# A hybrid SSD and attention layer: products with the states made channel-major, decays as rows from DRAM, the skip inside the decay matrix

## The chip, the cores and the metric

The kernel runs on one core of one Trainium2 chip. The metric is the device time of one execution in microseconds (us), lower is better. Three runs of the kernel before took 1216.43, 1216.73 and 1217.33 us, so the median is 1216.73 us. In the profile PE is the matrix engine TensorE, PEld its loading of weights, DVE is VectorE, ACT is ScalarE, POOL is GpSimd and SP is SyncE, which here issues most of the DMAs.

## The reference

One layer over 512 latent tokens with 1024 channels, and 256 context tokens that are only read. A combined projection feeds two mixers, an SSD (state space) branch that runs in both directions and a windowed attention, which are gated, merged, projected and followed by a gated ConvFFN. The change concerns only the output of the SSD branch. It has 32 heads of 64 channels in 4 groups, a state of 128 and chunks of 128 tokens:

```python
    decay_to_end = jnp.exp(cs[..., -1:] - cs)
    states = jnp.einsum('bcsgn,bgrcs,bcsgrp->bcgrpn', bc, decay_to_end, xc)
    ...
    cb = jnp.einsum('bclgn,bcsgn->bgcls', cc, bc)
    scores = cb[:, :, None] * jnp.exp(segsum(ac))
    y_diag = jnp.einsum('bgrcls,bcsgrp->bclgrp', scores, xc)
    y_off = jnp.einsum('bclgn,bcgrpn,bgrcl->bclgrp', cc, states[:, :-1], jnp.exp(cs))
    return (y_diag + y_off).reshape(Bsz, L, G, R, P).astype(xs.dtype), final
...
    y = yf + jnp.flip(yb, axis=1) if with_output else None
...
    y = y + d_skip.reshape(SSD_GROUPS, SSD_HPG, 1).astype(y.dtype) * xs
    return rmsnorm(y.reshape(Bsz, L, D_SSD) * jax.nn.silu(z), g)
```

For every chunk and group there are thus three parts: what the tokens of the chunk give each other (`y_diag`, in both directions), what the forward and the backward state give, each scaled by a decay per token and head (`y_off`), and the skip `d_skip * xs`. Their sum is multiplied by silu(z).

## The kernel before

The large products run on PE in three passes of a float32 split into a high and a low part (`gemm`, L238, L239, L241); the weights come by SP's queue into `wraw` (L177), ACT casts the high part `whi` (L183) and DVE subtracts for the low part `wlo` (L184). Before the SSD stand the modulation, the attention with most other projections beside it, and a stage that works out the decay tables: `tables` makes the cumulative sums `cs`, their exponential `U` (ACT) and more; `table_turns` turns `dt`, `U`, `X` and `la` so that tokens lie on partitions (three PE transposes each and two copies on ACT), into `TT`, `TU`, `TX` and `TD`. `cs` also goes to DRAM (`cs_d`).

The SSD itself lasts from about 430 to 720 us. The list `prog` takes the four groups one after the other and puts one projection of the next group (in the last group, a gate projection) behind each chunk: states, then for chunk c = 0 to 3 `chunk_out(c)`, `chunk_in(c+1)` and one projection step. A scheduler then orders the instructions of each engine, within what the program's dependencies allow; small pieces in the list `BETWEEN` are set by hand into the middle of a projection.

- `chunk_in(c)` prepares the decay matrices. Two DMAs broadcast rows of `cs_d` into `fb`. `products` makes B·C for the chunk on PE (`cb`, L1664), takes its diagonal on DVE (`cbd`, L1666) and makes `coef` on POOL (L1670, L1671): the diagonal of the backward direction plus the skip, one number for each token and head. `decays` adds on ACT (L1680, L1683), joins both directions on DVE (L1684) and takes the exponential on ACT (L1687) into two tiles `E` of four heads each. `weighed` multiplies `E` by `cb` on DVE (L1691). In three of four chunks (0 + 1 + 1 + 2 times a group) it also issues `square`: ACT squares a finished tile of the group before (L1558) into one buffer, and POOL adds it to `ssq` (L1559).
- `chunk_out(c)` makes two products with the states on PE, tokens on partitions (L1707: C is the stationary operand, the state with 512 columns moves through), which DVE scales by `TU` into two tiles `te` (L1709). Sixteen passes (L1715) make `yd`, channels on partitions, from `xs` and `E`. POOL makes `dx = xs*coef` (L1717) and adds both `te` (L1718, L1720). Then the state moves on (POOL L1581, PE L1579, DVE L1582). `late` adds `dx` to `yd` by four PE transposes (L1728) that accumulate in PSUM, and DVE multiplies by z (L1730).

A plain float32 product of PE shows as two passes in the trace, each with its own load of weights; a transpose is one pass.

## Time and profile before

| | |
|---|---|
| median of three runs | 1216.73 us |
| span of the profiled execution (first to last instruction) | 1215.7 us |
| TensorE clock granted in it | 1.000 |
| bytes moved by DMA | 215.74 MB, 177 GB/s on the mean |
| SSD part, 440 to 720 us: POOL busy | 116.4 of 280 us |
| SSD part: DVE busy | 221.2 of 280 us |

The profile gives no time of the profiled execution beside its span. The median of the runs lies 1.0 us above that span, and 1.0 us is taken as what lies around it. Busy time is counted from an instruction's start to its end, and the ends of the matrix engine's passes are modelled. What a pass costs is therefore read from the distance between two starts.

### The profile page before, as it was taken

The numbers are of one execution on the slowest core, as the hardware profiler recorded it, in microseconds if no ns is written. First come the engines' busy times: TensorE is split into PE (matmuls) and PEld (weight loads), VectorE is DVE, ScalarE is ACT, GpSimd is POOL, SyncE is SP. The second block draws the span as 40 slices with busy tenths as digits, with TensorE's granted clock in tenths as the row PEclk, the third lists the DMA queues.
The fourth block names the chain that finished last, engine by engine and source line by source line (L and its number), as shares of the span: only waits on it lengthen the run. The fifth ranks groups of instructions, "written<-read, shape, count | busy, mean of one in ns | idle before, by whom it ended". The sixth has DMA issues, their size and how long they took to land.

```text
span 1215.7 us, 17471 instructions
## 1 busy us (share of the span) xinstructions
PE 1208.4 (99%) x6288; PEld 992.9 (82%) x6288; DVE 923.6 (76%) x1494; ACT 683.4 (56%) x1269; POOL 220.9 (18%) x242
## 2 busy tenths in 40 slices
PE   9999999999999999999999999999999999999998
PEld 6798888888878877778787778888988888888886
DVE  5857888888565688697896867677687777778787
ACT  5557787778544367476575664223543443436654
POOL 0000121100102534252451622000200100110021
PEclk9999999999999999999999999999999999999999
DMA  9655889834758525356366558777266634436662
GB/s 371 258 139 184 160 239 263 170 139 137 170 154 257 172 85 175 116 128 202 96 160 207 171 186 273 242 232 249 51 161 149 194 118 135 133 105 222 214 185 98
DMA packets 124424, 215.74 MB, mean 177 GB/s; under 512 B 26697, under 2 KB 69745, under 8 KB 124337
## 3 DMA queue, kind: packets, MB, share of 16 engines
q1 hardware_dynamic: 110256, 187.09, 49.1%
q0 software_dynamic: 13792, 27.27, 9.9%
q8 instruction: 49, 0.80, 0.3%
q14 instruction: 39, 0.31, 0.1%
q10 hardware_dynamic: 288, 0.27, 0.1%
HBM read 187.78 MB, written 44.89 MB: 191 GB/s over the span
## 4 chain that ended last, share of the span: by engine, by line
PE 98%; issue 1%; DVE 0%; ACT 0%; POOL 0%; DVEq 0%; POOLq 0%; ACTq 0%
PE acc L238 20%; PE acc L241 20%; PE acc L239 20%; PE score L978 3%; PE po L1027 3%; PE pt L1014 2%; PE mis L581 2%; PE mis L1707 2%; PE mis L1579 2%; PE mis L2244 2%; PE mis L2245 2%; PE mis L2243 2%; PE mis L1715 1%; PE acc L2244 1%; PE acc L2245 1%; PE acc L2243 1%
## 5 line engine op out<-in xcount | busy, mean ns | idle before, releaser
L183 ACT CAST whi<-wraw 128x1024 fp32r<-128x1024 f32 (+1 forms) x115 | 120.3, 1047 | 159.3 <-PE acc L239 104.7
L184 DVE TENSOR_TENSOR wlo<-wraw,whi 128x1024 fp32r<-128x1024 f32 (+1 forms) x115 | 144.7, 1259 | 68.2 <-ACT whi L183 65.8
L238 PE MATMUL acc<-hlh,whi 128*128 128x512 f32 x472 | 193.9, 411 | 0.0
L239 PE MATMUL acc<-hll,whi 128*128 128x512 f32 x472 | 184.9, 392 | 0.0
L241 PE MATMUL acc<-hlh,wlo 128*128 128x512 f32 x472 | 184.9, 392 | 0.0
L241 PE MATMUL acc<-mh,wlo 128*128 128x512 f32 x368 | 143.3, 389 | 0.0
L238 PE MATMUL acc<-mh,whi 128*128 128x512 f32 x368 | 143.3, 389 | 0.0
L239 PE MATMUL acc<-ml,whi 128*128 128x512 f32 x368 | 143.2, 389 | 0.0
L241 PEld LDWEIGHTS acc<-hlh,wlo 128*128 128x128 f32 x472 | 88.6, 188 | 19.5
L238 PEld LDWEIGHTS acc<-hlh,whi 128*128 128x128 f32 x472 | 88.8, 188 | 17.9 <-issue 2.8
L239 PEld LDWEIGHTS acc<-hll,whi 128*128 128x128 f32 x472 | 88.9, 188 | 17.4 <-issue 2.4
L241 PEld LDWEIGHTS acc<-mh,wlo 128*128 128x128 f32 x368 | 69.1, 188 | 14.9 <-DVE wlo L184 0.5
L239 PEld LDWEIGHTS acc<-ml,whi 128*128 128x128 f32 x368 | 69.1, 188 | 14.4
L238 PEld LDWEIGHTS acc<-mh,whi 128*128 128x128 f32 x368 | 69.1, 188 | 14.2
L987 DVE CUSTOM_DVE_ANT_0 p<-score,winm,nsink 128x512 f32<-128x512 f32 (+1 forms) x64 | 51.8, 810 | 15.3 <-PE score L978 13.8
L1412 DVE SCALAR_TENSOR_TENSOR ta<-acc,half,ta 128x511 f32<-128x511 f32 (+1 forms) x66 | 43.8, 664 | 23.2 <-ACT ta L1411 23.0
L164 POOL DMA_DIRECT2D dsum<-wdn x24 | 25.4, 1146 | 193.1 <-DVE wlo L1111 171.8
L1411 ACT ACTIVATE ta<-acc,half 128x512 f32<-128x512 f32 (+1 forms) x66 | 46.8, 710 | 24.3 <-PE acc L241 23.0
L994 ACT ACTIVATE p<-p,mneg 128x512 f32<-128x512 f32 (+1 forms) x64 | 49.7, 777 | 15.4 <-DVE mneg L987 14.8
L1022 DVE TENSOR_TENSOR ptl<-pt,pth 128x512 fp32r<-128x512 f32 x72 | 47.5, 685 | 8.7 <-ACT pth L1018 7.7
L238 PE MATMUL acc<-hch,whi 128*128 128x256 f32 x176 | 53.2, 302 | 0.0
L812 DVE SCALAR_TENSOR_TENSOR tm<-wraw,csil,tm 128x512 f32<-128x512 f32 x56 | 43.1, 770 | 12.7 <-DMA wraw<-wm 12.0
(454 smaller groups left out, 3011.1 us busy)
## 6 DMA issues: line engine op xcount, KB each, us to landing
wraw<-wup SPq DMA_DIRECT2D x44, 512.0 KB, 3.8
dsum<-wdn POOLq DMA_DIRECT2D x24, 704.0 KB, 8.7
wraw<-wm SPq DMA_DIRECT2D x32, 512.0 KB, 3.6
fb<-cs_d SPq DMA_DIRECT2D x32, 512.0 KB, 6.6
wraw<-wx SPq DMA_DIRECT2D x24, 512.0 KB, 3.6
wm<-wm SPq DMA_DIRECT2D x16, 512.0 KB, 8.3
wraw<-wz SPq DMA_DIRECT2D x16, 512.0 KB, 4.3
wraw<-wos SPq DMA_DIRECT2D x16, 512.0 KB, 4.7
```

What stands on the lines that cost most here:

```text
L183: F["cast"] = S.copy(hi[:, :n], r[:, :n])
L184: F["sub"] = V.tensor_tensor(lo[:, :n], r[:, :n], raw(hi[:, :n]), ALU.subtract)
L238: T.matmul(ps, wh, xh[:, k0 + k, :], start=a, stop=False)
L239: T.matmul(ps, wh, xl[:, k0 + k, :], start=False, stop=False)
L241: T.matmul(ps, wl, xh[:, k0 + k, :], start=False, stop=b)
L812: V.scalar_tensor_tensor(acc, r[:, u * 512 : u * 512 + 512], sc, acc, ALU.mult, ALU.add)
L987: V.tensor_tensor_reduce(p[:, :w], d["ps"][i][:, o0 : o0 + w], m, op0=ALU.add, op1=ALU.min, scale=1.0, scalar=nsink[:, h : h + 1], accum_o ...
L994: S.activation(p, p, AF.Exp, bias=d["mneg"][:, i : i + 1], scale=-1.0, accum_out=d["den"][:, i : i + 1])
L1022: V.tensor_tensor(d["ptl"][x], d["pt"][x], raw(d["pth"][x]), ALU.subtract)
L1411: S.activation(o[:, :n], ps[:, :n], AF.Identity, scale=hcol(base_w, stride + i), bias=hcol(base_b, i))
L1412: x = V.scalar_tensor_tensor(o[:, 1:n], ps[:, 0 : n - 1], hcol(base_w, i), o[:, 1:n], ALU.mult, ALU.add)
L2243: T.matmul(ps, h, wh, start=st, stop=False, skip_group_check=True)
```

## The change

Three things are done for every chunk and group.

The products with the states are made with channels on partitions. Each becomes four products with 128 columns of the state as the stationary operand and C as the moving one (L1738 in the changed kernel, in place of L1707). The decay per token must now lie along the free axis: `far_out` writes `U` to DRAM (`us_d`), and four DMAs a chunk read it back as rows, each broadcast over 64 partitions, into two tiles `far` (three buffers). The table `TU`, its three transposes and its two copies go.

For chunks 1 to 3 `coef` enters the decay matrix: POOL makes two tiles `dg` (identity times `coef`) and, behind DVE's `weighed`, adds them to `E`. The four transposes of `late` then go; chunk 0 keeps `dx` and its transposes. POOL's two adds of `te` become one (`y`), DVE adds `yd` to it, and the multiplication by z moves from DVE to POOL.

The scratch of the software DMA queue (POOL's) is set to 4096 bytes a partition. Left out of the diff: the new DRAM tile, the list of table turns without `U`, and the tile `TU`.

```diff
+        def far_out():
+            for a in range(2):
+                for x in range(2):
+                    (r0, r1), n = rows(a, x), 128 if x else 384
+                    nc.sync.dma_start(us_d[32 * a : 32 * a + 32, 384 * x : 384 * x + n], d["U"][r0:r1, :n])
...
-        op("20", "ACT", 1.8, act("U", "cs", AF.Exp), ["17", "e1"])
+        op("20", "ACT", 1.8, lambda: (act("U", "cs", AF.Exp)(), far_out()), ["17", "e1"])
...
+            far = []
+            for dr in range(2):
+                f = bp.tile([P, 4, P], F32, tag="far", name="far", bufs=FAR)
+                for u in range(2):
+                    a = bass.AP(
+                        tensor=us_d.tensor,
+                        offset=us_d.offset + (32 * dr + 8 * g + u) * L + c * P,
+                        ap=[[0, 64], [2 * L, 4], [1, P]],
+                    )
+                    nc.sync.dma_start(f[64 * u : 64 * u + 64], a)
+                far.append(f)
+            d["far", c] = far
...
+                d["dg"] = [diagonal(q) for q in range(2)] if c else None
+
+            def diagonal(q):
+                dg = bp.tile([P, 4, P], F32, tag="dg", name="dg", bufs=2)
+                w = d["coef"][:, 4 * q : 4 * q + 4].unsqueeze(2).to_broadcast([P, 4, P])
+                G.tensor_tensor(dg, ident.unsqueeze(1).to_broadcast([P, 4, P]), w, ALU.mult)
+                return dg
...
-                for E in d["E"]:
+                for q, E in enumerate(d["E"]):
                     V.tensor_tensor(E, E, d["cb"][:, :P].unsqueeze(1).to_broadcast([P, 4, P]), ALU.mult)
+                    if c:
+                        G.tensor_tensor(E, E, d["dg"][q], ALU.add)
...
-                T.matmul(ps, d["CT"][:, tok], s, start=True, stop=True)
+                for ct in range(4):
+                    z = slice(ct * P, (ct + 1) * P)
+                    T.matmul(ps[:, z], s[:, z], d["CT"][:, tok], start=True, stop=True)
                 t = tmp("te")
-                V.tensor_tensor(h8(t), h8(ps), bc64(TU[:, c, dr, 8 * g : 8 * g + 8]), ALU.mult)
+                V.tensor_tensor(t, ps, flat(far[dr]), ALU.mult)
...
-            dx = bp.tile([P, 512], F32, tag="tf", name="dx", bufs=1)
-            G.tensor_tensor(h8(dx), h8(xs[:, c, :]), bc64(coef), ALU.mult)
-            G.tensor_tensor(dx, dx, parts[1], ALU.add)
-            y = dx
-            G.tensor_tensor(dx, dx, parts[0], ALU.add)
+            dx = None
+            if not c:
+                dx = bp.tile([P, 512], F32, tag="dx", name="dx", bufs=1)
+                G.tensor_tensor(h8(dx), h8(xs[:, c, :]), bc64(d["coef"]), ALU.mult)
+            y = bp.tile([P, 512], F32, tag="tf", name="y", bufs=1)
+            G.tensor_tensor(y, parts[0], parts[1], ALU.add)
...
-                for ct in range(4):
+                for ct in range(0 if c else 4):
                     z = slice(ct * P, (ct + 1) * P)
-                    tc.keep_in_program_order(T.matmul(yd[:, z], y[:, z], ident, start=False, stop=ct == 3, is_transpose=True))
+                    tc.keep_in_program_order(T.matmul(yd[:, z], dx[:, z], ident, start=False, stop=ct == 3, is_transpose=True))
+                V.tensor_tensor(y, yd, y, ALU.add)
                 z = d["zt"][:, :, tok]
-                V.tensor_tensor(z, yd.rearrange("p (a t) -> p a t", a=4), z, ALU.mult)
+                G.tensor_tensor(z, y.rearrange("p (a t) -> p a t", a=4), z, ALU.mult)
...
-    nc = bacc.Bacc("TRN2", target_bir_lowering=False, num_devices=1)
+    nc = bacc.Bacc("TRN2", target_bir_lowering=False, num_devices=1, dynamic_dma_scratch_size=4096)
```

The order of the built program shows where the new instructions stand. On PE, in the last group between chunks 2 and 3, before:

```order
L239 MATMUL acc<-hll,whi 128x512
L241 MATMUL acc<-hlh,wlo 128x512
L1728 MATMUL mis<-ident,dx 128x128 x4
L1707 MATMUL mis<-st,CT 128x512 x2
L1715 MATMUL mis<-E,xs 64x128 x8
L238 MATMUL acc<-hlh,whi 128x512
```

and in the changed kernel, at the same place:

```order
L239 MATMUL acc<-hll,whi 128x512
L241 MATMUL acc<-hlh,wlo 128x512
L1738 MATMUL mis<-CT,st 128x128 x8
L1746 MATMUL mis<-E,xs 64x128 x8
L238 MATMUL acc<-hlh,whi 128x512
```

The four transposes are gone, and two products with 512 columns have become eight with 128. The products with `E` (L1746) now follow an add on POOL.

On POOL, in the third group (group 2), from the adds of chunk 1's `te` to those of chunk 2's, before:

```order
L1718 TENSOR_TENSOR dx<-dx,te 128x512
L1720 TENSOR_TENSOR dx<-dx,te 128x512
L1559 TENSOR_TENSOR ssq<-ssq,sq 128x512
L1581 TENSOR_TENSOR st<-st,eT 128x512
L1670 TENSOR_SCALAR coef<-TT,cbd 128x8
L1671 TENSOR_TENSOR coef<-coef,bcs 128x8
L1559 TENSOR_TENSOR ssq<-ssq,sq 128x512 x2
L1717 TENSOR_TENSOR dx<-xs,coef 128x512
L1718 TENSOR_TENSOR dx<-dx,te 128x512
```

and in the changed kernel:

```order
L1752 TENSOR_TENSOR y<-te 128x512
L1567 TENSOR_TENSOR ssq<-ssq,sq 128x512
L1589 TENSOR_TENSOR st<-st,eT 128x512
L1690 TENSOR_SCALAR coef<-TT,cbd 128x8
L1691 TENSOR_TENSOR coef<-coef,bcs 128x8
L1697 TENSOR_TENSOR dg<-ident,coef 128x512 x2
L1763 TENSOR_TENSOR zs<-y,zs 128x4x128
L1567 TENSOR_TENSOR ssq<-ssq,sq 128x512
L1720 TENSOR_TENSOR E<-E,dg 128x512 x2
L1567 TENSOR_TENSOR ssq<-ssq,sq 128x512
L1752 TENSOR_TENSOR y<-te 128x512
```

Between `coef` and the next `te` two `dg`, a multiplication by z and two adds to `E` have come in; the adds to `E`, which PE needs, stand behind z's and behind one of `ssq`.

On SP, in the same group from chunk 1 to chunk 2, before:

```order
L177 DMA wraw<-wg 128x1024
L1657 DMA fb<-cs_d 128x8x128 x2
L177 DMA wraw<-wm 128x1024
L1636 DMA zs<-zs_d 128x512 x4
L1657 DMA fb<-cs_d 128x8x128
```

and in the changed kernel:

```order
L177 DMA wraw<-wg 128x1024
L1665 DMA fb<-cs_d 128x8x128 x2
L1676 DMA far<-us_d 64x4x128 x4
L177 DMA wraw<-wm 128x1024
L1644 DMA zs<-zs_d 128x512 x4
L1665 DMA fb<-cs_d 128x8x128
```

The four DMAs of `far`, two for chunk 3's second tile and two for the next group's first, stand between the broadcast rows and the next weights.

More of the change, by code (lines that the diff above doesn't have):

```diff
@@ L267, in tile_hybrid_layer @@
     cs_d = dpool.tile([64, L], F32, name="cs_d")
+    us_d = dpool.tile([64, L], F32, name="us_d")
     dt_d = dpool.tile([64, L + LC], F32, name="dt_d")
@@ L1389, in tile_hybrid_layer @@
         tabp = bpool.enter_context(tc.tile_pool(name="tabp", bufs=1, reuse_waits="tile"))
-        TX, TU = (tabp.tile([P, 4, 2, 32], F32, name=n) for n in ("TX", "TU"))
+        TX = tabp.tile([P, 4, 2, 32], F32, name="TX")
         TD = tabp.tile([P, 6, 2, 32], F32, name="TD")
@@ L1701, in chunk_out @@
         def chunk_out(c):
-            xs, coef, E = d["xs"], d["coef"], d["E"]
+            xs, E, far = d["xs"], d["E"], d.pop(("far", c))
             tok = slice(c * P, (c + 1) * P)
@@ L1714, in chunk_out @@
                 o = yd[64 * (h % 2) : 64 * (h % 2) + 64, (h // 2) * P : (h // 2 + 1) * P]
[L1715 to L1720 removed]
+                T.matmul(o, xs[:, c, h * 64 : (h + 1) * 64], E[h // 4][:, h % 4, :], start=h < 2, stop=c > 0 and h > 5)
+            dx = None
[4 more added lines that the diff above has]
+            G.tensor_tensor(y, parts[0], parts[1], ALU.add)
             if c < 3:
```

4 lines of the change are left out of this document (2 added, 2 removed).

## The prediction

> **What bounds the kernel now.** I read the page's busy times first, then the chain that ended last by engine, then windows over single steps of the SSD, and then the timelines of the engines in one step.
>
> ```profile
> PE 1208.4 (99%) x6288; PEld 992.9 (82%) x6288; DVE 923.6 (76%) x1494; ACT 683.4 (56%) x1269; POOL 220.9 (18%) x242
> PE 98%; issue 1%; DVE 0%; ACT 0%; POOL 0%; DVEq 0%; POOLq 0%; ACTq 0%
> ```
>
> PE is busy nearly always and carries 98% of the chain. So a pass taken from PE is worth its full time, and any wait given to PE costs its full time. The question is whether another engine now makes PE wait. A step is the time from one chunk's products with the states to the next chunk's. The windows give the step's length, then the busy time of PE, PEld, DVE, ACT and POOL with the instructions, the clock, the DMA share and GB/s:
>
> ```profile
> 611.52:624.98 13.46, 13.46 (x84) 10.59 (x83) 12.73 (x19) 10.70 (x27) 8.65 (x9) 1.00 0.58 122
> ...
> 700.14:710.06 9.92, 9.92 (x53) 7.02 (x52) 6.05 (x10) 6.83 (x17) 3.99 (x5) 1.00 0.34 109
> ```
>
> PE has no gap in either. POOL has 4.8 and 5.9 us to spare, DVE in the longer step only 0.7.
>
> **What goes on PE.** Chunks 1 to 3 of four groups lose four transposes each, and the table stage loses three:
>
> ```profile
> 609.80 0.60 PE L1728 MATMUL mis<-ident,dx 128*128 128x128 f32 x4
> 610.23 0.38 PE L1441 MATMUL mis<-ident,tc 128*128 128x128 f32 x2
> ...
> 352.39 0.49 PE L1324 MATMUL pt<-ident,dU 128*128 128x128 f32 x3
> 352.72 0.49 PE L1324 MATMUL pt<-ident,dX 128*128 128x128 f32 x3
> ```
>
> From start to next start, four transposes take 610.23 - 609.80 = 0.43 us and three turns take 0.33. That is 12 x 0.43 + 0.33 = 5.5 us removed.
>
> **What comes on PE.** Each of 32 products becomes four with 128 columns, eight passes for two. The first two rows are of the timeline, the others of the chain in order of time:
>
> ```profile
> 8.04 1.58 PE L459 MATMUL mis<-ones 128*128 128x128 f32 x12
> 9.38 0.72 PE L581 MATMUL mis<-ah,w0h 128*128 128x512 f32 x2
> ...
> 598.65 1.72 PE mis L1707 x4
> 600.37 1.02 PE mis L1715 x16
> ```
>
> Twelve plain float32 passes with 128 columns take 1.34 us, 0.112 each, so eight take 0.89. Today's two passes take 1.72 / 2 = 0.86. The difference of 0.03 to 0.04 us over 32 products is 1.15 us. At the transposes' pace (0.43 / 4 = 0.107) it would be nothing, so 0 to 1.2; I take 1.15, since those rows are products too. PE's sum is then -5.5 + 1.15 = **-4.3 us** (-5.5 to -4.3).
>
> **What comes ahead of PE on POOL.** Today `E` is ready once DVE has weighed it, well before PE needs it (3.6 us in chunk 3 of group 2, whose rows are below). Now POOL must first take `coef`, make two `dg`, and add them to `E`. As the order shows, z's multiplication and one `ssq` stand ahead of these adds in chunk 2 of groups 1 and 2. Group 2's rows of today:
>
> ```profile
> 616.86 2.16 POOL L1720 TENSOR_TENSOR dx<-dx,te 128x512 f32<-128x512 f32 x1
> ...
> 620.42 1.07 POOL L1581 TENSOR_TENSOR st<-st,eT 128x512 f32<-128x512 f32 x1
> 621.47 0.32 POOL L1670 TENSOR_SCALAR coef<-TT,cbd 128x8 f32<-128x8 f32 x1
> 621.87 0.20 POOL L1671 TENSOR_TENSOR coef<-coef,bcs 128x8 f32<-128x8 f32 x1
> ...
> 624.07 1.29 POOL L1559 TENSOR_TENSOR ssq<-ssq,sq 128x512 f32<-128x512 f32 x1 [0.74 <-ACT sq L1558]
> 625.32 1.04 POOL L1717 TENSOR_TENSOR dx<-xs,coef 128x512 f32<-128x512 f32 x1
> ```
> ```profile
> 619.23 0.67 DVE L1582 TENSOR_TENSOR st<-st,mis 128x512 f32<-128x512 f32 x1
> ...
> 620.03 0.13 DVE L1666 DVE_READ_ACCUMULATOR2_ANT cbd<- 128x1 f32 x1
> ```
> ```profile
> 626.80 1.09 PE L1715 MATMUL mis<-E,xs 128*64 128x128 f32 x16
> ```
>
> A plain add of 128x512 takes 1.29 us (L1559), one with a broadcast factor 1.04 (L1717). No row shows `dg`, whose two inputs are both broadcast; the nearest row is L1717, so 1.05, between 0.32 (that form at 128x8) and 1.29.
>
> - DVE's `st` ends at 619.90. POOL's `st` (1.07) and `coef` (0.32 + 0.20 and gaps) follow: 621.6. One add of `te` fewer does not bring this forward further, since DVE's `st` ends last.
> - Two `dg` (2.1): 623.7. z (1.29): 625.0. `ssq` (1.29): 626.3.
> - The two adds to `E` end at 627.6 and 628.9.
> - PE wants the first `E` at 626.80 less the 0.43 of the lost transposes, 626.4, and the second eight passes later, half of 1.02, at 626.9. The second is late by **2.0 us**.
>
> Group 1 has the same POOL order, 79.5 us earlier, and there ACT is the later one:
>
> ```profile
> 542.36 0.20 POOL L1671 TENSOR_TENSOR coef<-coef,bcs 128x8 f32<-128x8 f32 x1
> ...
> 546.10 0.57 ACT L1537 COPY xs<-mis 128x512 f32<-128x512 f32 x1
> ...
> 547.72 1.09 PE L1715 MATMUL mis<-E,xs 128*64 128x128 f32 x16
> ```
> ```profile
> 623.36 0.63 ACT L1558 ACTIVATE sq<-zs 128x512 f32<-128x512 f32 x1 [0.22 <-POOL ssq L1559]
> 623.90 1.26 ACT L1680 ACTIVATE E<-fb,TX 128x128 f32<-128x128 f32 x4
> ```
>
> `coef` ends 0.45 earlier than today as in group 2, at 542.1; `dg` 544.2, z 545.5, `ssq` 546.8. ACT's third `sq` has one buffer and waits for that `ssq`. Queued behind it on ACT are four exponent adds (1.26) and the copy `xs` (0.57), by which PE's passes with `E` wait in this group for their PSUM: 546.8 + 0.55 + 1.26 + 0.57 = 549.2, where PE wants it at 547.72 - 0.43 = 547.3. Late by **1.9 us**.
>
> In the ten other steps I made the same sum. In six or seven it leaves 0.5 us or more. Chunk 3 of group 2 stands for these:
>
> ```profile
> 632.19 0.13 DVE L1666 DVE_READ_ACCUMULATOR2_ANT cbd<- 128x1 f32 x1
> 636.50 0.69 DVE L1691 TENSOR_TENSOR E<-E,mis 128x512 f32<-128x512 f32 x1 [0.25 <-ACT E L1687]
> ...
> 640.28 0.98 PE L1715 MATMUL mis<-E,xs 128*64 128x128 f32 x14
> ```
>
> From `cbd` (632.3) come `coef` 632.9, `dg` 635.0, z 636.3, the adds 637.6 and 638.9; PE wants the second at 640.28 - 0.43 + 0.51 = 640.4, so 1.5 us are left. The tightest is chunk 1 of group 3, with two `ssq` about `y`:
>
> ```profile
> 676.45 1.30 POOL L1559 TENSOR_TENSOR ssq<-ssq,sq 128x512 f32<-128x512 f32 x1 [2.90 <-ACT sq L1558]
> ...
> 686.51 1.09 PE L1715 MATMUL mis<-E,xs 128*64 128x128 f32 x16
> ```
>
> From 677.8: `y` 679.1, `ssq` 680.5 (at 1.4), `st` 681.6, `coef` 682.2, `dg` 684.3, adds 685.6 and 686.9, against 686.51 - 0.43 + 0.51 = 686.6: late by 0.3.
>
> POOL's adds do not always take 1.29:
>
> ```profile
> 615.66 2.21 DVE L184 TENSOR_TENSOR wlo<-wraw,whi 128x1024 fp32r<-128x1024 f32 x1
> ...
> 627.13 1.23 DVE L184 TENSOR_TENSOR wlo<-wraw,whi 128x1024 fp32r<-128x1024 f32 x1 [0.22 <-ACT whi L183]
> ```
> ```profile
> L1720 POOL TENSOR_TENSOR dx<-dx,te 128x512 f32<-128x512 f32 x16 | 25.1, 1568 | 1.1
> L1717 POOL TENSOR_TENSOR dx<-xs,coef 128x512 f32<-128x512 f32 x16 | 16.7, 1045 | 23.6 <-PE mis L1728 23.2
> ```
>
> The add at 616.86 lies beside `wlo`, and both are long: 2.16 for 1.29, and 2.21 for 1.23. Such a hold costs POOL 0.87. But the sixteen L1717, which stand late in a step where the adds to `E` will stand, average 1.045: no hold there. So for the ten steps I take one hold, at the tight place: 0.3 + 0.87 = **1.2 us** (0 to 6, ten steps with a hold of 0.6 each). All waits together: 2.0 + 1.9 + 1.2 = 5.1.
>
> [...]
>
> **Costed at nothing.** SP's transfers have time:
>
> ```profile
> fb<-cs_d SPq DMA_DIRECT2D x32, 512.0 KB, 6.6
> ```
> ```profile
> 620.31 0.98 SPq L1657 DMA_DIRECT2D fb<-cs_d  x2
> 628.39 0.34 SPq L177 DMA_DIRECT2D wraw<-wm  x1
> ```
> ```profile
> 351.44 0.37 SPq L177 DMA_DIRECT2D wraw<-wx  x1
> 354.19 0.34 SPq L1271 DMA_DIRECT2D tb<-tt_d  x1
> ```
>
> - A tile of `far` is as large as one `fb` (512 KB over 128 partitions in two halves against 6.6 us to land) and is issued a chunk ahead (the shorter step above is 9.92 us). Its issue waits for the `te` that frees its buffer; behind it on SP stands `wraw<-wm`, which moves from 628.4 to about 631.5 by my estimate; DVE's sum with it now stands behind the weighing that ends at 637.2, and that covers it. Without the cover it would cost the 3 us of the shift.
> - In the table stage four stores of `U` go ahead of the weights at 351.44. These move behind the table read, to about 354.6, and are cast only when the two loads ahead are used up: 0, at most the 3.2 us of the shift.
> - DVE's `te` reads `far` in place of `TU` at the same size, and `y` replaces z's multiplication. DVE's path keeps its length.
> - The smaller scratch of POOL's queue is seen in no row: 0, and at most one such landing of 6.6 us.
>
> **Rivals.**
>
> - *A: POOL keeps up.* POOL's `st`, z and `ssq` come early enough since one add of `te` (1.3 us) has gone, and PE never waits. For it: POOL is busy 18%. Against it: DVE's `st` at 619.90, not POOL's load, sets when `coef` can start. It gives 1216.7 - 4.3 = 1212.4.
> - *B: slower, by holds between DVE and POOL.* One hold of 0.87 us meets the chain from `coef` to the second `E` in every step. The two late steps then cost 3.9 + 1.7, the tight one 1.2, and the nine others what exceeds their spare of 0 to 2 us, about 1.9: 8.7 in all, 1216.7 - 4.3 + 8.7 = 1221.1. It is slower from waits of 6.8 us on. For it: DVE is busy 12.73 of 13.46 us in such a step. Against it: L1717's mean of 1.045.
> - *C: SP's queue.* The late `wm` or `far` holds DVE in each group: 1 to 2 us more, 1219.0.
>
> The diff could also fail to do what it says only in part: chunk 0 keeps its 16 transposes, as the order shows, and these are not in my sum.
>
> **How the numbers follow.** The profiled execution has a span of 1215.7 and 1.0 us around it, 1216.7, equal to the median. -4.3 + 5.1 = +0.8 gives **1217.5 us**, with 1214.5 to 1219.5 as its own range. Chances: forecast 0.45, A 0.24, B 0.27, C 0.04. The range, with A's lower bound (-5.5) and B with two holds in some steps, is 1211.4 to 1223.0. About 0.2% (2.4 us) is what a measurement here can tell from no change. A and a little of the forecast are faster (0.26); most of the forecast is the same (0.43); B, and the upper ends of the forecast and C, are slower (0.31).
>
> **What would show it.** The transposes of L1728 fall to 16, and eight passes of the new product take 0.89. PE's rows show a wait of about 2 us ahead of the products with `E` in chunk 2 of groups 1 and 2, released by POOL's `E` or ACT's `xs`, and next to none in chunk 3. No such wait: A. Waits in most steps, beside POOL adds of 1.5 to 2.2: B. A wait on `far`, `wraw` or `tm` would be C, and one on a load by POOL's queue would prove the scratch's price wrong.

## The result, and the profile after

The changed kernel takes 1232.97 us (median of 4 runs, 1230.09 to 1233.33) where the kernel before takes 1216.97 beside it (median of 4). The ratio is 1.0124 (95% interval 1.0110 to 1.0138): 16 us slower, and outside the range of the forecast (1211.4 to 1223.0). The profiled execution has a span of 1231.4 us and took 1233.18, so what lies around a span is 1.8 us and not the 1.0 that the prediction took; that shifts both kernels alike. One of the ten executions of e16, in the table of experiments below, took 1720.13 us at a granted clock of 0.654; it counts in e16's median (1220.45; 1220.29 without it) but not in its ratio.

First the page's busy times and the chain of the changed kernel, then PE's waits by line (us in total, times, longest):

```profile
PE 1209.4 (98%) x6429; PEld 1009.0 (82%) x6429; DVE 932.3 (76%) x1494; ACT 682.3 (55%) x1267; POOL 266.7 (22%) x278
...
PE 81%; DVE 7%; issue 3%; DMA 3%; POOL 3%; ACT 2%; SPq 0%; DVEq 0%; ACTq 0%; POOLq 0%
```
```profile
PE mis L1746 <- POOL E L1720: 10.0, 7, 3.7
PE mis L1606 <- DVE xw L1575: 3.2, 1, 3.2
```

The chain, 98% on PE before, is now 81% on PE. PE's busy time did not fall by 4.3 us but rose by 1.0 (1208.4 before). Two things have to be explained: PE's waits in the SSD (13.2 us in the two lines shown, 13.6 with one of 0.4 for a turn of `tc`), and passes that got longer. PE's timeline shows the waits in brackets:

```profile
549.61 1.09 PE L1746 MATMUL mis<-E,xs 128*64 128x128 f32 x16 [2.99 <-POOL E L1720]
...
631.12 0.66 PE L1746 MATMUL mis<-E,xs 128*64 128x128 f32 x8 [1.00 <-POOL E L1720]
632.35 0.66 PE L1746 MATMUL mis<-E,xs 128*64 128x128 f32 x8 [0.58 <-POOL E L1720]
645.31 0.66 PE L1746 MATMUL mis<-E,xs 128*64 128x128 f32 x8 [0.25 <-POOL E L1720]
646.99 0.66 PE L1746 MATMUL mis<-E,xs 128*64 128x128 f32 x8 [1.02 <-POOL E L1720]
671.44 1.98 PE L1606 MATMUL mis<-xw,Bkc 128*128 128x512 f32 x4 [3.18 <-DVE xw L1575]
724.33 0.81 PE L1746 MATMUL mis<-E,xs 128*64 128x128 f32 x8 [3.72 <-POOL E L1720]
725.55 1.12 PE L1746 MATMUL mis<-E,xs 128*64 128x128 f32 x8 [0.41 <-POOL E L1720]
```

These are chunk 2 of group 1, chunks 2 and 3 of group 2, the start of group 3 (another product) and chunk 3 of group 3. The windows behind three of them (PE, PEld, DVE, ACT, POOL, then the granted clock, the DMA share and GB/s):

```profile
550.30:554.00 3.70, 3.65 (x15) 2.04 (x12) 3.70 (x8) 2.49 (x7) 0.54 (x1) 0.54 0.02 4
...
671.50:676.00 4.50, 4.50 (x15) 2.87 (x16) 1.87 (x3) 1.28 (x2) 1.06 (x1) 1.00 0.68 262
...
724.30:729.00 4.70, 4.25 (x22) 3.05 (x23) 2.26 (x4) 2.28 (x4) 3.86 (x3) 0.54 0.53 174
```

Behind the waits of 2.99 and 3.72 us the granted clock is 0.54; behind the one of 3.18 it stayed at 1.00. Summed over windows of 2 us, (1 - clock) x 2, the low clock costs 5.1 us: 1.7 in group 1 and 3.4 at the end. With the saved passes, -4.3 + 5.1, that is about the rise of PE's busy time.

The table gives the step from the start of one chunk's products with the states to the next one's, in us, and its difference from before. It is worked out from PE's timelines; the kernels after the second column are experiments below. "2,3" runs into group 3, and "end" goes from the last chunk to the end of the span.

```
g,c    before   changed        e1            e9            e15           e17
0,0     13.04  13.09 +0.05  13.09 +0.05  13.10 +0.06  13.09 +0.05  13.08 +0.04
0,1     13.46  13.10 -0.36  13.54 +0.08  13.10 -0.36  13.54 +0.08  13.10 -0.36
0,2     13.47  13.10 -0.37  13.53 +0.06  13.09 -0.38  13.53 +0.06  13.10 -0.37
0,3     39.11  38.79 -0.32  39.32 +0.21  38.80 -0.31  39.23 +0.12  38.81 -0.30
1,0     13.02  13.09 +0.07  13.09 +0.07  13.09 +0.07  13.09 +0.07  13.09 +0.07
1,1     13.89  13.53 -0.36  13.98 +0.09  13.53 -0.36  13.98 +0.09  13.54 -0.35
1,2     13.44  17.84 +4.40  13.98 +0.54  14.66 +1.22  13.53 +0.09  14.79 +1.35
1,3     39.15  39.48 +0.33  39.32 +0.17  39.92 +0.77  39.22 +0.07  40.12 +0.97
2,0     13.04  13.08 +0.04  13.08 +0.04  13.10 +0.06  13.09 +0.05  13.09 +0.05
2,1     13.46  13.10 -0.36  13.55 +0.09  13.10 -0.36  13.54 +0.08  13.10 -0.36
2,2     13.47  14.95 +1.48  13.53 +0.06  13.73 +0.26  13.53 +0.06  14.07 +0.60
2,3     35.88  40.56 +4.68  37.62 +1.74  37.30 +1.42  35.95 +0.07  37.23 +1.35
3,0     10.35  10.44 +0.09  10.44 +0.09  10.43 +0.08  10.44 +0.09  10.44 +0.09
3,1     15.46  14.99 -0.47  15.49 +0.03  15.04 -0.42  15.50 +0.04  15.02 -0.44
3,2      9.91   9.56 -0.35  10.01 +0.10   9.56 -0.35  10.00 +0.09   9.56 -0.35
end    505.64 512.74 +7.10 507.70 +2.06 508.68 +3.04 506.35 +0.71 506.39 +0.75
```

Where nothing waits, a step with its transposes removed is 0.36 shorter and one that keeps them 0.04 to 0.09 longer: the sum of PE's passes was right. All of the loss lies in chunks 2 and 3 of groups 1 and 2 and in the end. Chunk 2 of groups 1 and 2 waits where the prediction said. In group 1 POOL and ACT end almost together:

```profile
547.12 2.49 POOL L1720 TENSOR_TENSOR E<-E,dg 128x512 f32<-128x512 f32 x2
```
```profile
548.90 0.56 ACT L1545 COPY xs<-mis 128x512 f32<-128x512 f32 x1
```

The second add ends at 549.61 and lets PE go; ACT's `xs`, which the prediction had as the later one, ends at 549.46. Three other chains lead to the rest.

**The last chunk of group 3.** The rows of POOL, ACT, DVE and PE, one fence each:

```profile
707.19 4.02 POOL L1720 TENSOR_TENSOR E<-E,dg 128x512 f32<-128x512 f32 x2
711.18 1.27 POOL L1567 TENSOR_TENSOR ssq<-ssq,sq 128x512 f32<-128x512 f32 x1
...
718.52 0.20 POOL L1691 TENSOR_TENSOR coef<-coef,bcs 128x8 f32<-128x8 f32 x1
...
722.02 3.48 POOL L1720 TENSOR_TENSOR E<-E,dg 128x512 f32<-128x512 f32 x2
```
```profile
712.48 0.63 ACT L1566 ACTIVATE sq<-zs 128x512 f32<-128x512 f32 x1 [5.45 <-POOL ssq L1567]
...
713.30 1.03 ACT L183 CAST whi<-wraw 128x1024 fp32r<-128x1024 f32 x1
```
```profile
714.37 1.23 DVE L184 TENSOR_TENSOR wlo<-wraw,whi 128x1024 fp32r<-128x1024 f32 x1 [4.28 <-ACT whi L183]
715.51 1.28 DVE L1740 TENSOR_TENSOR te<-mis,far 128x512 f32<-128x512 f32 x2
...
717.51 0.14 DVE L1686 DVE_READ_ACCUMULATOR2_ANT cbd<- 128x1 f32 x1
```
```profile
718.66 1.95 PE L1738 MATMUL mis<-CT,st 128*128 128x128 f32 x16
```

Read in order of time: POOL adds to the previous chunk's `E`, then to `ssq`; only now is `sq`'s one buffer free, and ACT, which stood 5.45 us, goes on; the cast behind it lets DVE go on, which stood 4.28; then come `te`, `st` and `cbd`. `cbd` is done 1.0 us ahead of PE's products, where before it was 4.9 ahead (done at 705.2, products at 710.06). So `coef`, `dg`, z and the adds start late, and PE waits 4.1 us in all.

**The start of group 3.** SP's queue and DVE's:

```profile
655.79 2.78 SPq L1774 DMA_DIRECT2D yz_d<-zs  x4
...
660.53 0.48 SPq L177 DMA_DIRECT2D wraw<-wm  x1
```
```profile
668.11 1.54 DVE L813 SCALAR_TENSOR_TENSOR tm<-wraw,csil,tm 128x512 f32<-128x512 f32 x2 [5.10 <-DMA wraw<-wm]
...
670.70 1.28 DVE L1575 TENSOR_TENSOR xw<-xsc,TD 128x512 f32<-128x512 f32 x2
```

`wm` is issued behind the stores of z, which wait for POOL's z. `tm` waits 5.10 us for `wm`, and behind it in DVE's queue stands `xw`, for which PE waits. The stores alone don't explain the wait: before, `wm` also stood behind them and landed 3.6 us after its issue; here it took 7.6 us, with an `fb` and two loads of z issued between the stores and it. With z on DVE again (e13 below) `tm` waits as long:

```profile
667.10 1.54 DVE L813 SCALAR_TENSOR_TENSOR tm<-wraw,csil,tm 128x512 f32<-128x512 f32 x2 [5.33 <-DMA wraw<-wm]
```

So POOL's z alone is not what makes `wm` late; which transfer does was not tried apart.

**Chunk 3 of group 2**, where the prediction saw 1.5 us to spare:

```profile
629.87 0.63 ACT L1566 ACTIVATE sq<-zs 128x512 f32<-128x512 f32 x1 [2.49 <-POOL ssq L1567]
```
```profile
632.70 1.37 DVE L1429 SCALAR_TENSOR_TENSOR tc<-tb,ta 128x512 f32<-128x512 f32 x1 [3.75 <-ACT tb L1428]
...
642.95 2.86 DVE L813 SCALAR_TENSOR_TENSOR tm<-wraw,csil,tm 128x512 f32<-128x512 f32 x2 [0.22 <-DMA wraw<-wm]
```
```profile
643.54 3.39 POOL L1720 TENSOR_TENSOR E<-E,dg 128x512 f32<-128x512 f32 x2
```

ACT's hold in the step before reaches DVE (3.75 us), so this step's `cbd` is late; then two adds to `E` and two sums `tm` lie beside each other and take 3.39 and 2.86 us, where two plain adds take 2.6 and two `tm` 1.54 (first DVE row of group 3's start). `tm` lies there because `wm` came late on SP:

```profile
635.10 2.57 SPq L1676 DMA_DIRECT2D far<-us_d  x4
638.72 0.35 SPq L177 DMA_DIRECT2D wraw<-wm  x1
```

Before, this `wm` was issued at 628.39, 3.4 us behind chunk 2's products; here it is 10.6 us behind them, after `far`.

### The profile page after: what moved, and what is told of

Same layout as the page of the kernel before. It is cut to its first block, busy times and chain, and to the rows that moved or that the text cites. A ratio compares the mean times of both kernels' runs of the same rounds, so it can differ in the third digit from the quotient of the medians.

```text
span 1231.4 us, 17909 instructions
## 1 busy us (share of the span) xinstructions
PE 1209.4 (98%) x6429; PEld 1009.0 (82%) x6429; DVE 932.3 (76%) x1494; ACT 682.3 (55%) x1267; POOL 266.7 (22%) x278
## 4 chain that ended last, share of the span: by engine, by line
PE 81%; DVE 7%; issue 3%; DMA 3%; POOL 3%; ACT 2%; SPq 0%; DVEq 0%; ACTq 0%; POOLq 0%
PE acc L238 17%; PE acc L239 17%; PE acc L241 17%; PE score L979 3%; PE po L1028 3%; PE pt L1015 2%; PE mis L582 2%; PE mis L2278 2%; PE mis L2276 2%; PE mis L2277 2%; DMA wraw<-wm 1%; PE acc L2278 1%; PE acc L2276 1%; PE acc L2277 1%; PE acc L1098 1%
## 5 line engine op out<-in xcount | busy, mean ns | idle before, releaser
L238 PEld LDWEIGHTS acc<-mh,whi 128*128 128x128 f32 x368 | 69.1, 188 | 14.4
L813 DVE SCALAR_TENSOR_TENSOR tm<-wraw,csil,tm 128x512 f32<-128x512 f32 x56 | 46.3, 827 | 17.1 <-DMA wraw<-wm 16.4
L1418 ACT ACTIVATE ta<-acc,half 128x512 f32<-128x512 f32 (+1 forms) x66 | 46.6, 707 | 17.0 <-PE acc L241 15.7
```

Source lines behind the costliest of these rows:

```text
L238: T.matmul(ps, wh, xh[:, k0 + k, :], start=a, stop=False)
L813: V.scalar_tensor_tensor(acc, r[:, u * 512 : u * 512 + 512], sc, acc, ALU.mult, ALU.add)
L1418: S.activation(o[:, :n], ps[:, :n], AF.Identity, scale=hcol(base_w, stride + i), bias=hcol(base_b, i))
```

## The experiments

The letters here are not those of the prediction's rivals. Theory A: the adds to `E` come late on POOL, and the low clock follows the waits. B: `far`'s transfers on SP make weights late. C: z on POOL holds DVE. Added on the way: D, `xw` queued behind `tm`; E, `sq`'s one buffer holds ACT; F, z on POOL delays the ends of the groups; G, z one operation further behind PE delays its stores at the end. Each ratio is to the kernel before on the same chip, with its 95% interval; waits are PE's between 430 and 770 us, and "low clock" is summed as above.

| kernel | median, us | ratio | waits | low clock |
|---|---|---|---|---|
| changed | 1232.97 | 1.0124 (1.0110 to 1.0138) | 13.6 | 5.1 |
| e1 no adds to E, transposes back | 1222.12 | 1.0042 (1.0028 to 1.0056) | 2.6 | 0 |
| e2 adds left out | 1228.24 | 1.0090 (1.0075 to 1.0105) | 9.5 | 6.8 |
| e3 z behind the adds | 1229.91 | 1.0105 (1.0090 to 1.0120) | 11.6 | 3.4 |
| e4 PE filled | 1235.72 | 1.0149 (1.0134 to 1.0165) | 12.4 | 5.1 |
| e5 xw ahead of tm | 1229.29 | 1.0095 (1.0080 to 1.0110) | 9.8 | 5.1 |
| e6 two buffers of sq | 1225.95 | 1.0066 (1.0050 to 1.0083) | 11.5 | 1.7 |
| e7 = e3 + e5 + e6 | 1223.89 | 1.0054 (1.0039 to 1.0069) | 8.0 | 1.7 |
| e8 = e7 + ssq behind the adds | 1228.13 | 1.0088 (1.0073 to 1.0103) | 11.9 | 0 |
| e9 = e7 with `dx` beside `sq`, far behind wm | 1221.60 | 1.0035 (1.0023 to 1.0047) | 6.3 | 0 |
| e10 adds in eight steps, e5 | 1222.98 | 1.0049 (1.0037 to 1.0062) | 5.3 | 1.7 |
| e11 = e10 + e9's edits | 1222.43 | 1.0043 (1.0030 to 1.0055) | 4.6 | 1.7 |
| e12 = e1 + z on DVE, e5 | 1222.23 | 1.0042 (1.0028 to 1.0056) | 2.5 | 0 |
| e13 changed, z on DVE | 1230.60 | 1.0108 (1.0094 to 1.0122) | 12.2 | 3.4 |
| e14 = e9 + z on DVE in chunk 3 | 1222.35 | 1.0038 (1.0024 to 1.0052) | 7.0 | 1.7 |
| e15 = e12 + y joined on PE at the end | 1219.18 | 1.0016 (1.0007 to 1.0025) | 0.0 | 0 |
| e16 = e9 + y joined on PE at the end | 1220.45 | 1.0023 (1.0014 to 1.0033) | 5.2 | 0 |
| e17 = e15 + adds in eight steps | 1220.44 | 1.0032 (1.0021 to 1.0043) | 3.2 | 0 |
| e18 = e17 + two buffers of sq, far behind wm | 1219.57 | 1.0021 (1.0012 to 1.0030) | 2.7 | 0 |

### e1 and e2: take the adds away

```diff
-                    if c:
-                        G.tensor_tensor(E, E, d["dg"][q], ALU.add)
```

e1 also drops `dg` and makes `dx` and the transposes in every chunk. e2 drops only these two lines, so it leaves out the skip and the backward diagonal in chunks 1 to 3; it is there for its time alone.

> Undoes the second part alone: coef goes through dx and the four transposes in every chunk again, the products stay channel-major, far, y and z stay as in the changed kernel. Theory A (the late adds to E on POOL are the loss, by PE's waits for E and by the lower granted clock behind long waits): no wait of PE for E, no drop of the granted clock, and the time is the PE sum without the removed transposes, 1216.7 - 0.33 + 1.15 = 1217.5 us, 1216.5 to 1219. Rival B (the DMAs of far on SP's queue make weights late): the wait of 3.2 us ahead of the context sum of group 3 stays, 1220 to 1222. Rival C (z on POOL holds DVE): waits of 1 us or more in several steps, above 1222.

> Leaves out the adds of dg to E in chunks 1 to 3, and with them the skip and the backward diagonal of these chunks; dg is still made, all else stays. Theory A: PE's waits for E go, 10 us, and the 5 us of lower clock behind them, and PE keeps the passes that it saved: 1216.7 - 4.3 = 1212.4 us, 1211 to 1215. Rival B: the wait of 3.2 us ahead of the context sum stays: 1215.6 us. If it stays above 1220, the adds to E are not the cause.

Both came out above what theory A said, e1 by 4.6 us and e2 by 16. In e2 not one add to `E` is left. The waits in chunk 3 of group 2 and in the last chunk are gone (the end is 0.5 us over before), but in chunk 2 of groups 1 and 2 PE still waits, now for ACT (PE's timeline, then ACT's):

```profile
549.88 1.09 PE L1744 MATMUL mis<-E,xs 128*64 128x128 f32 x16 [2.90 <-ACT xs L1545]
...
632.98 1.60 PE L1587 MATMUL mis<-xw,Bk 128*128 128x512 f32 x2 [2.00 <-ACT xs L1545]
```
```profile
547.56 0.63 ACT L1566 ACTIVATE sq<-zs 128x512 f32<-128x512 f32 x1 [2.47 <-POOL ssq L1567]
```

So in chunk 2 of these groups the adds are only the last link: `dg` and z, ahead of `ssq` on POOL, hold ACT through `sq`. The wait at group 3 stays (3.83 us). Theory A alone is refuted; C's waits in several steps did not come in e1, whose longest wait is 1.15 us.

### e3, e5, e6, e13: one order, one buffer or one engine at a time

e3 keeps the adds to `E` and z in program order on POOL, which puts z behind them. e5 puts `tm` behind `xw` on DVE (`x` is the instruction of `tm`). e6 gives `sq` two buffers, and `dx` a buffer of `dg`'s to make room. e13 moves z to DVE. The cuts, in the order e3 (one of its two lines), e5, e6, e13:

```diff
-                        G.tensor_tensor(E, E, d["dg"][q], ALU.add)
+                        tc.keep_in_program_order(G.tensor_tensor(E, E, d["dg"][q], ALU.add))
...
+                if i == 7:
+                    tc.add_manual_dep(x.ins, F["ctx"].ins.name, QUEUED, reason="behind the context")
...
-            sq = tmp("ta") if last else zp.tile([P, 512], F32, tag="th", name="sq", bufs=1)
+            sq = tmp("ta") if last else zp.tile([P, 512], F32, tag="th", name="sq", bufs=2)
...
-                G.tensor_tensor(z, y.rearrange("p (a t) -> p a t", a=4), z, ALU.mult)
+                (V if True else G).tensor_tensor(z, y.rearrange("p (a t) -> p a t", a=4), z, ALU.mult)
```

> Only the order on POOL changes: z's multiplication stands behind the two adds to E wherever it stood ahead of them; the same work on every engine. Theory A: E comes 1.3 us earlier in the steps that wait, so PE's waits for E of 3.0, 1.6, 1.3 and 4.1 us fall to about 1.7, 0.3, 0 and 2.8, and with waits under 3 us the granted clock drops less: 1233 - 5.2 = 1227.8 us, or 1223 to 1225 if both drops of the clock go too. Rival (ACT, held by the single sq buffer, ends last, not z): the waits hardly change in the first and the last of the four places, 1230 to 1232.

> One order on DVE changes: at the start of group 3 the two weighings of the context (xw) stand ahead of a modulation sum (tm) that waited 5.1 us for its weights wm. Theory D (PE's wait of 3.2 us ahead of the context sum comes from that queue, since wm was issued late on SP behind the stores of z): the wait goes, 1233.0 - 3.2 = 1229.8 us, 1228.5 to 1231. If xw itself was late for another reason: 1232 to 1234.

> ACT's sq gets a second buffer (dx lies in dg's place to make room). Theory E (the third sq of a step waits for POOL's ssq and holds ACT's queue, so that the weight split, te, coef and at last E of the last chunk come late): the wait of 4.1 us in chunk 3 of group 3 falls under 1.5, with it the 3.4 us of low clock behind it; in chunk 2 of group 1 E stays late by POOL alone, 2.5 to 3.0 us: 1225 to 1228 us. If POOL's own chain sets E there too: 1231 to 1233.

> The changed kernel with z's multiplication back on DVE in every chunk, nothing else. POOL has 1.29 us less ahead of the adds to E, DVE 0.68 more. Theories A and F: the waits for E fall by about as much as with z behind the adds (10 to 5), and the end of the SSD comes about 2 us earlier: 1226 to 1229 us. If DVE cannot take it (it is busy 12.7 of 13.5 us in a step): 1230 to 1234.

e5 and e6 did what they were made for. In e5 the wait of 3.18 us is gone and the time is 3.7 lower: D holds. In e6 the last chunk no longer waits for `E` at all, and no low clock follows there; the time is 7.0 lower, as E says. In chunk 2 of groups 1 and 2 two waits of 1.0 to 1.3 us are left in each: 2.0 us in all where it was 3.0, and 2.4 where it was 1.6. Two new waits came, 0.9 us in chunk 1 of group 3 and 2.2 us behind the SSD, the second with a low clock. e3 missed in time, though its wait in chunk 2 of group 1 fell to 1.8 us as expected: waits for `E` fell from 10.0 to 5.6, but the wait at group 3 cost more (2.8 us and now a low clock behind it), and PE waited 2.1 us for turns of `tc` that DVE made late. e13 landed where its expectation put the case that DVE cannot take z: its waits for `E` fell to 4.2 us, and `xs`, turns of `tc` and `xw` (3.4 us with a low clock) took their place. A wait taken away at one place came back in part at another in each of them.

### e4: more work on PE instead of a wait

```diff
-                for ct in range(4):
+                for ct in [0, 1, 2, 3] * (3 if dr and (g, c) in ((1, 2), (3, 3)) else 1):
```

> In the two steps with the longest waits for E (chunk 2 of group 1, chunk 3 of group 3) the second product with the state is made three times over, 16 more passes or 1.8 us of PE work each, ahead of the waiting instruction. If the granted clock falls because PE stands still too long, the waits of 3.0 and 4.1 us shrink to 1.2 and 2.3, the clock stays at 1.00 behind them, and more work on PE makes the kernel 2 to 5 us faster: 1228 to 1231 us. If the low clock has nothing to do with the wait's length, or costs nothing on the path: 1233 us or more (up to 1236, since te comes 1.8 us later in two steps).

In chunk 2 of group 1 it is as expected: the wait is 1.22 us, the clock stays at 1.00, and the step takes 17.12 us where the changed kernel takes 17.84, with 1.8 us more work in it. The next step, whose `te` comes later, is 1.45 us longer and takes that back. In group 3 it is not: the last chunk still waits 1.91 and 0.56 us and the clock falls, and the wait for `xw` now has a low clock behind it. As a whole the kernel is slower, at the upper end of what its expectation gave to the other case; as a test of the clock, one place speaks for it and one says nothing.

### e7, e8, e9, e14: the edits together

e8 issues each `ssq` behind the adds of its step. e9 puts `dx` beside `sq` in place of `dg`'s buffer, and each `far` of groups 1 to 3 behind the last `wm`. e14 has z of chunk 3 on DVE.

```diff
-                dx = bp.tile([P, 512], F32, tag="dx", name="dx", bufs=1)
+                dx = zp.tile([P, 512], F32, tag="th", name="dx", bufs=2)
...
+                    if g and M_LOADS:
+                        tc.add_manual_dep(dma.ins, M_LOADS[max(M_LOADS)].ins.name, QUEUED, reason="behind a load")
```

> z behind the adds to E, two buffers of sq, and xw ahead of tm together; one ssq still stands ahead of the adds in two steps. Theories A, D and E together: waits of PE of at most 0.5 us in each of those two steps, no wait of 2 us and so no low clock: 1216.7 - 4.3 + 1 to 3 = 1213.5 to 1215.5 us. If the loss lies elsewhere (DVE held by POOL, transfers): above 1219.

> As the kernel with three edits, and every ssq of a step stands behind its adds to E too. Theories A, D and E: no wait of PE for E, ACT's xs or xw at all, clock at 1.00: the sum of PE's passes alone, 1216.7 - 4.3 = 1212.4 us, 1211.5 to 1214. If the change gains nothing even without these waits, or ssq only moves a wait to ACT: 1216 or more.

> The kernel with three edits again, with dx in a buffer beside sq in place of dg's (there dg waited 1.1 us for the transposes of dx in chunk 1 of group 3, and PE 1.7 us with a drop of the clock), and each far issued behind the last modulation weights. Theories A, D and E: that step loses its +3.2 and is -0.4 as in the changed kernel, 1223.9 - 3.6 = 1220.3 us, 1218.5 to 1221.5, with no granted clock under 0.97. If the low clock has another cause than the wait: it stays somewhere, above 1222.

> The three edits (clean version, 1221.6) with z's multiplication on DVE in the last chunk of each group. Theory F: the wait of 1.35 us for rs at the end and part of the +3.0 of the end go, z's stores come 0.8 to 2 us earlier in each group: 1219 to 1220.5 us, still not below before, since the waits for E of 1.2 and 1.3 us and for the turns stay. If z is not what delays the ends: 1221 to 1222.5.

None reached its sum. In e7 one loss was of my own making, the shared buffer (POOL's timeline, chunk 1 of group 3):

```profile
686.23 1.04 POOL L1700 TENSOR_TENSOR dg<-ident,coef 128x512 f32<-128x512 f32 x1 [1.06 <-PE mis L1763]
```

e9 without it has that step at -0.42 and no low clock. e8 is a miss and tells most: with every `ssq` out of the way it is 4 us slower than e7, waits for turns of `tc` (1.8 and 1.6 us) and for `E` taking the place of those removed. e14 gained nothing over e9, against theory F.

### e10 and e11: the adds only where PE did not wait

```diff
+        def on(c):
+            return c > 0 and (g, c) not in ((1, 2), (2, 2), (2, 3), (3, 3))
```

`on(c)` takes the place of `c` in `dg`, in the adds and in the transposes.

> The adds to E are kept in the eight steps in which PE did not wait for them, and coef goes through dx and the transposes again in the four in which it did (chunk 2 of group 1, chunks 2 and 3 of group 2, chunk 3 of group 3); xw ahead of tm. Theory A (only late adds to E, not the adds as such, cost): PE's sum is -0.33 + 1.15 - 8 x 0.43 = -2.6, so 1214.1 us if nothing else waits; the kernel without any add to E was 4.6 above its PE sum, 1.2 of it by xw, so up to 3.4 more: 1214 to 1217.5 us, and in any case at least 3 us under the kernel without adds (1222.1). If the adds to E cost where PE does not wait for them at once (by holds of DVE): no better than that kernel, 1220 or more.

> The selection of the eight steps together with z behind the adds, two buffers of sq, xw ahead of tm and far behind the modulation weights. If the edits add up: 1213 to 1216 us. If two buffers of sq or z behind the adds only move the waits to the turns of the next group's projection, as with four edits: 1217 to 1220.

Neither is better than e1: e10 lands where its expectation put the case that the adds cost even in these steps, e11 above both of its ranges. In chunk 2 of group 1 PE waits 1.94 and 1.96 us for ACT's `xs`, with a low clock behind it, and in chunk 3 of group 2 1.82 and 1.34 us for ACT's `tb`, although neither step has an add to `E`. In group 1 ACT's `sq` waited 1.50 us for `ssq` in both. e11 is no clean test of two buffers there, since `dx` of these four steps lies in the same two buffers as `sq` (tag `th` in the cut above).

### e12, e15, e16: the end of the SSD

e1 still had some 3 us that its passes and the wait for `xw` don't explain, 2.06 of it at the end. z there is two operations behind PE, not one. e12 has z on DVE. e15 and e16 join `y` to `yd` on PE in the very last chunk, so that z follows PE at once, as before:

```diff
+                if (g, c) == (3, 3):
+                    tc.keep_in_program_order(T.matmul(yd, ident, y, start=False, stop=True))
+                    z = d["zt"][:, :, tok]
+                    V.tensor_tensor(z, yd.rearrange("p (a t) -> p a t", a=4), z, ALU.mult)
+                    return
```

> Channel-major products alone: coef through dx and transposes in every chunk, z's multiplication back on DVE (behind y), xw ahead of tm. The kernel without adds was 4.6 us above its PE sum; its z of the last chunk was ready 2.6 us later after the last transposes than before the change, and the stores and loads behind it made PE wait at the end. Theory F (z on POOL is a second, separate loss at the ends of the groups, xw the third): PE sum 1217.5 and at most 1.5 more, 1217.5 to 1219.0 us, end of the SSD within 0.7 us of before. If far's transfers or the passes themselves cost it: 1220.5 to 1222.

> As the channel-major products alone (z on DVE, xw ahead of tm), but in the very last chunk y joins yd by one product with the identity on PE (0.46 us), so that z is one operation behind PE again. Theory G (the extra step between the last products and z delays z's stores and the reloads behind them, and PE waits at the end): the end of the SSD, 3.6 us over before, comes to 0.5 to 1.3 over: 1222.2 - 2.5 = 1219.7 us, 1218.5 to 1220.5. If the end is late for another reason (far on SP, other orders): 1221.5 to 1223.

> The clean kernel with three edits (1221.6) and the same join on PE in the very last chunk. Theory G: its end, 3.0 us over before, loses 2 to 2.5, 1219.0 to 1220.5 us. To be faster than before it would have to lose the waits for E in three steps (1.2, 0.4, 1.3 us) and for the turns (1.1 us) as well. If G is wrong: 1221 to 1222.5.

e12 missed as a whole, but its steps up to the end are all at their sum (+0.04 to +0.13), so `far`'s transfers cost nothing there (theory B falls), and all that is left is the end. With z on DVE it is 3.6 us late, later than in e1 with z on POOL (2.06), so theory F falls too. DVE's rows of e12, then ACT's and PE's:

```profile
719.18 0.69 DVE L1762 TENSOR_TENSOR y<-mis,y 128x512 f32<-128x512 f32 x1 [4.95 <-PE mis L1761]
719.79 1.22 DVE L184 TENSOR_TENSOR wlo<-wraw,whi 128x1024 fp32r<-128x1024 f32 x1
720.92 0.69 DVE L1764 TENSOR_TENSOR zs<-y,zs 128x512 f32<-128x512 f32 x1
```
```profile
728.63 0.72 ACT L1819 ACTIVATE yh<-ld,vec 128x512 fp32r<-128x512 f32 x1 [2.43 <-DMA ld<-yz_d]
```
```profile
741.98 0.50 PE L241 MATMUL acc<-yh,wlo 128*128 128x512 f32 x1 [1.24 <-DVE wlo L184]
```

z is done at 721.6; before, it was done at 719.8 on almost the same time line. It goes to DRAM and is read back, and ACT waits 2.43 us for that (0.91 before). With `y` joined on PE (e15) the end is +0.71, and no wait is left in the SSD or behind it. G holds: the end gains 2.9 us over e12. In e16 it gains 1.1 us over e9, half of what was expected; there PE still waits 1.3 us for `E` in the last chunk.

### e17 and e18: do the adds gain where they come in time?

> The kernel in which no step waited (channel-major products, z on DVE, xw ahead of tm, y joined on PE in the very last chunk; 1219.2) with the adds to E put in again in the eight steps in which PE did not wait for them. If these adds are free where PE does not wait: 8 x 0.44 = 3.5 us less, 1215.7 us (1214.5 to 1217), equal to before or just faster. If POOL's adds hold DVE or ACT there too, so that another wait comes (in the selection before, ACT's xs in chunk 2 of group 1, 1.9 us and a drop of the clock): 1218 to 1220.

> The same with two buffers of sq and far behind the modulation weights. If sq's wait for ssq on POOL is what makes ACT's copies late in chunk 2 of group 1: that wait goes, and it is 1214.5 to 1216.5 us. If not: as the kernel without these two edits, within 1 us.

They don't. In e17 seven steps with the adds are at -0.30 to -0.44, near the forecast -0.36. But three other waits come (PE's timeline):

```profile
546.89 1.09 PE L1752 MATMUL mis<-E,xs 128*64 128x128 f32 x16 [0.85 <-ACT xs L1547]
...
562.03 1.09 PE L1752 MATMUL mis<-E,xs 128*64 128x128 f32 x16 [1.19 <-DVE y L1772]
...
642.41 1.09 PE L1752 MATMUL mis<-E,xs 128*64 128x128 f32 x16 [1.20 <-ACT tb L1430]
```

Two of these steps have no add to `E` themselves. The eight adds save 3.5 us of passes and cost 3.2 us of waits and a slower chunk 2 of group 2 (+0.60): 1220.4 against 1219.2 for e15. e18's edits take back 0.6 of the middle wait. No version was faster than before; the nearest is e15, 0.16% above it, without any add to `E`. By its passes it could not be faster: by the estimates above, eight passes for two add 1.15 us, the join 0.46 (719.57 to 720.03 us in e15), and the table stage saves 0.33.

## Why the prediction was wrong

- **PE's passes: right in the steps.** -0.43 + 0.07 a step was forecast and -0.36 measured, +0.07 for the products and 0.04 to 0.12 measured in e15. The 0.33 us of the table stage can't be told: PE reaches the first products with the states at 439.91 us before and at 438.75 to 440.31 in the kernels behind it, all of which have the shorter stage. (The lower end of the range, by the -5.5 that it names, is 1211.2 and not 1211.4.)
- **Two late steps, 1.9 and 2.0 us: the right mechanism at the right places, badly sized.** They are 3.0 and 1.6 us. In group 1 the forecast had PE at 547.3 and its input at 549.2; PE was there at 546.6, since it had gained in the steps before too, and `E` came at 549.6. `coef` was not 0.45 earlier, as forecast: z on POOL and `tc` on DVE had lain beside each other (1.74 us for `tc`, 0.69 before), and DVE's `st` behind them came 0.5 later. The forecast compared POOL's times with PE's of before, less one step's gain.
- **"In the ten other steps I made the same sum" is the step that failed.** It took each step's `cbd` from the trace of before, as though a late step left the next one alone. The hold on ACT by `sq`, which the prediction saw only for `xs` in group 1, goes on through ACT's queue to DVE, and from there to the next `te`, `st` and `cbd`. Chunk 3 of group 2 was to have 1.5 us to spare and was 1.3 late; chunk 3 of group 3 was late by 4.1. The tight place of the forecast, chunk 1 of group 3 with 1.2 us, did not wait at all. e6 gives `sq` its second buffer (and moves `dx` to make room): ACT's hold there falls from 5.45 to 3.19 us, and the last chunk's wait goes.
- **The clock was left out.** Every wait was priced at its length; two of them cost 5.1 us more. This part is read from the granted clock of the windows, and e4 supports it at one place. In eight kernels, the one before among them, the longest wait there is under 1.5 us, and their low clock is 0.
- **SP "costed at nothing" was wrong, in another place than named.** Where the prediction looked (chunk 2 of group 2), `wm` shifted by 7 us against PE and not by 3; `tm` waited only 0.22 us for it, but fell beside the adds to `E`. The next `wm`, behind z's stores, cost PE 3.2 us. The prediction's rival C, at 0.04, came nearest: a late `wm` holds DVE, though in group 3 alone; e5, which puts `tm` behind `xw`, shows it. The size was misread too: a tile of `far` is two halves of 128 KB, so half of one `fb` (512 KB) and not as large. No wait of PE is on a load of POOL's queue, so the scratch's 0 stands.
- **z's move from one operation behind PE to two was not in the sum.** No step in the middle of e12 shows a cost; at the end it is most of 2.1 us in e1 and of 3.6 in e12, of which e15 takes back 2.9. In the changed kernel itself the end was later by the wait for `E` and the clock (4.1 + 3.4, more than the 7.1 by which it is late), so there it stayed covered.
- **Holds (the prediction's rival B)** are there: 24 adds to `E` average 1.42 us (row below) where 1.29 was taken, and pairs beside `tm` or `wlo` take 3.4 to 4.0. They did not make PE wait in every step, as rival B said: eight of the twelve steps have no wait. Their share in the four late steps was not tried apart; an estimate from the rows, against 2.6 for a plain pair, is 0.8 of the 1.3 us in chunk 3 of group 2, and 0.9 of the 4.1 in the last chunk with 1.4 more in the pair ahead of its `ssq`.

In the terms of the forecast's sum: the two late steps 3.9 us forecast and 4.6 measured, the tight place 1.2 and 0, the nine other steps 0 and 5.4, SP 0 and 3.2, the clock 0 and 5.1; a turn of `tc` adds 0.4. Of the 15.7 us by which the span grew, waits are 13.6, the low clock 5.1 and the saved passes -4.3, which is 14.4. Of the 1.3 us left, 0.6 are waits of PE at the very start (1.7 against 1.0 us), which differ between the kernels; the rest is unassigned. In e18 ACT is late in group 1 because it waits 1.68 us for DVE's join of `E`, where before it waited 0.27; why DVE is late there stays open.

## What to carry to other kernels

Where one engine is busy 99% of the time, count how long before its need each input is ready in every step, and let a late step shift the next one: the queues behind a wait (here ACT behind a one-buffer scratch, 5.45 us, DVE behind a weight, 5.10 us) carry it on. Work that is moved off the bound engine and onto three that feed it has to fit their order, not their load: POOL was 18% busy, and PE still came to wait 10.0 us for its adds to `E`. An operation added ahead of a store that is soon read back can cost its time and its place in the queue at the end of the stage, as in e12 (3.6 us), even if it is hidden everywhere else, as in e12's other steps (+0.04 to +0.13).

## What the runs showed of the hardware

In the changed kernel the granted clock was 0.50 behind two waits of PE, of 2.99 and 3.72 us (windows 550.7 to 554.0 and 724.8 to 731.5 us), and 1.00 behind the one of 3.18 us (671.5 to 678.0). Over all kernels 16 single waits of PE in this part were 1.9 us or longer, and 14 of them had such a fall behind them; the two without it were 3.18 us (the changed kernel) and 3.07 us (e6). Of the shorter waits a fall came at four places, each with one of over 1.5 us, twice alone (1.54 us in e7, 1.55 us in e14) and twice with a second beside it; eight other waits of 1.5 to 1.8 us had none behind them. So the length alone does not decide: a wait of 1.54 us was enough in e7, and one of 3.18 us was not in the changed kernel. The 2 us in e7's expectation was an estimate that its own wait of 1.54 us does not bear out; the 3 us in e3's was one too, and e3's wait of 2.8 us had a fall behind it. What decides beside the length was not shown. Each fall cost 1.7 or 3.4 us by the windows, that is 3.4 or 6.8 us at half the clock.

Two groups of POOL in the SSD of the changed kernel (busy us and mean ns, then the idle time before them):

```profile
L1720 POOL TENSOR_TENSOR E<-E,dg 128x512 f32<-128x512 f32 x24 | 33.6, 1421 | 0.2 <-DVE E L1718 0.2
...
L1697 POOL TENSOR_TENSOR dg<-ident,coef 128x512 f32<-128x512 f32 x24 | 25.4, 1078 | 0.9
```

`dg`, with two broadcast inputs, takes 1.08 us, near the 1.05 that the prediction took from a product with one broadcast factor; the adds are on the mean 0.13 us longer than a plain one of 1.29.
